# The MLP's up projection as seven Strassen block products in two passes over the tokens, with the hidden layer taken through DRAM

## The chip, the cores and the metric

One Trainium2 chip, one of its cores. The metric is the device time of one execution in microseconds, the median over runs. Engines are named as in the profile: PE is TensorE's matmuls and PEld its weight loads, DVE is VectorE, ACT is ScalarE, POOL is GpSimd, SP is the engine on whose queue the DMAs are issued. SBUF is the on-chip memory, PSUM the banks that TensorE writes to.

## The reference

One layer of an encoder in float32, model width 1024, on 256 + 1024 = 1280 tokens. A norm and an input projection feed two branches (a state-space branch S5 and a two-directional Mamba-2 branch), whose outputs are gated, merged, projected and added to the input. Then comes the part that the change touches:

```python
x = x + (merged @ w_o)
h = rmsnorm(x, norm2_w)
x = x + jnp.square(jax.nn.relu(h @ w_up)) @ w_down    # w_up 1024 x 4096, w_down 4096 x 1024
```

and a last norm.

## The kernel before, in words

Data lie with channels on the 128 partitions and tokens along the free axis, so an activation of width 1024 is 8 blocks of 128 x 1280. Matmuls keep float32 accuracy by splitting both operands: hi is the value rounded to TensorE's format (an ACT copy), lo the rest (a subtraction), and each product is three matmuls, wl x hi, wh x lo, wh x hi. `mm3` (line 132) does that for one bank of PSUM; `mm3n` (139) does it for several chunks of tokens with the same weights, each matmul with a weight load of its own. `load_w` (113) fetches 4 blocks of weights (128 x 512, 256 KB) into a `raw` tile on SP's queue, casts them to `wh` on ACT (line 119) and subtracts for `wl` (line 120) on the engine that `lows` names in turn: POOL alone, and POOL and DVE in turn from line 761 to 775. There are four buffers of wh and of wl.

The stages at the end run in this order. The S5 output stage (lines 679 to 712) works on 320 tokens at a time. Then the tokens go through in three chunks of 432, 432 and 416 (`cs`, line 669). For each, `merge` (717) projects the Mamba branch and adds the gated S5 branch; `norm_rows` (753) makes the reciprocal norm `rs2` of the chunk before, by one matmul and a chain of DVE operations (`rsqrt`, 933); `normed` (655) prepares the next chunk; and `residual` (732) multiplies by w_o, adds the input to give x2, stores x2 to DRAM and leaves hi and lo of x2 times the norm's weights in `xn` (lines 743, 744). Squares are summed on ACT and POOL (749, 750). As rs2 is one factor per token, it is applied only after the up projection.

The MLP (780 to 816) goes over 16 blocks of 256 hidden channels. `up(b)` (783) makes two hidden tiles: 8 blocks of weights by three token chunks of 512, 512 and 256, i.e. 24 groups of three matmuls; DVE takes max(0, .) times rs2 out of PSUM (791); ACT squares that to hi (793), POOL squares it too (794) and DVE subtracts for lo (795). `down(b)` (799) multiplies the two tiles by w_down and DVE adds the result to `acc` (807), eight blocks of 128 x 1280 that start as x2, loaded back from DRAM. `up(b + 1)` is issued ahead of `down(b)`. The last two blocks of down, the last norm and the output stand in lines 818 to 930.

The order of the instructions on each engine is not written out here: a planner puts them in order at build time by the order of the program and by its own estimates of durations, with what stands in `urgent()` (106) ahead of the rest; at run time each queue is worked in order. Tiles of a pool that is closed leave their memory to later pools, whose writers then wait for the last readers. Banks of PSUM come in turn from eight (`any_bank`, 150).

## Time and profile before

| | |
|---|---|
| time, median of 3 runs | 2584.03 us (2583.57 to 2584.58) |
| the profiled execution: its time, its span | 2585.0 us, 2583.2 us |
| PE busy, share of the span | 2487.1 us, 96% |
| DVE, ACT, POOL busy | 1507.5, 948.6, 701.9 us |
| granted clock, mean over the span | 0.987 |
| merge and residual, up and down, last norm | 1376 to 1664.6, to 2507, to the end |

Busy shares are averages over stages. What an engine's work costs is read in its own stage: from what TensorE waits for there, and from the rate at which its matmuls start. A matmul's recorded duration overlaps with the next one's, so durations of PE don't add up; starts do. A recorded duration on DVE or POOL holds what the instruction waited for once it had begun.

### The profile page before, as it was taken

How to read it: one execution, taken by the hardware profiler on the slowest of the kernel's cores; microseconds unless marked ns; L12 is line 12 of the kernel's file. 1: busy time of each engine (PE TensorE's matmuls, PEld its weight loads, DVE VectorE, ACT ScalarE, POOL GpSimd, SP SyncE). 2: the span in 40 equal slices, each digit the busy share in tenths (PEclk: the TensorE clock that was granted, in tenths of full speed). 3: DMA queues.
4: the chain of work that ended last, by engine and by line, in shares of the span. 5: the costliest groups of instructions: out<-in, count | busy, mean ns of one | idle time of the engine just before them, and what ended most of it. 6: DMA issues, size and time to landing. Idle time of an engine off the chain costs nothing.

```text
span 2583.2 us, 37060 instructions
## 1 busy us (share of the span) xinstructions
PE 2487.1 (96%) x14119; PEld 2132.6 (83%) x14119; DVE 1507.5 (58%) x2505; ACT 948.6 (37%) x1867; POOL 701.9 (27%) x498
## 2 busy tenths in 40 slices
PE   8999999979999999988989999999999999999998
PEld 6788878868888888877889899988888888888887
DVE  7799999682456667668653665533233333333336
ACT  7555554333545545454332444311111111111114
POOL 2521111211111111134242424432222222222235
PEclk9999999989999999989999999999999999999999
DMA  4323232333344545565656766431111111111113
GB/s 148 102 84 100 90 99 92 102 103 125 132 136 155 163 133 165 148 180 149 194 173 193 232 188 202 143 121 37 39 39 37 37 37 41 38 37 37 37 45 115
DMA packets 254434, 286.21 MB, mean 111 GB/s; under 512 B 29864, under 2 KB 186704, under 8 KB 254256
## 3 DMA queue, kind: packets, MB, share of 16 engines
q1 hardware_dynamic: 252528, 279.90, 34.5%
q10 hardware_dynamic: 1728, 3.93, 0.5%
q8 instruction: 112, 1.84, 0.3%
q14 instruction: 66, 0.54, 0.1%
HBM read 210.26 MB, written 73.50 MB: 110 GB/s over the span
## 4 chain that ended last, share of the span: by engine, by line
PE 70%; DVE 17%; DMA 6%; ACT 3%; issue 2%; SPq 1%; POOL 1%; ACTq 0%; DVEq 0%; POOLq 0%
PE pa L145 24%; PE mm L136 20%; PE pa L136 9%; PE mm L145 8%; DVE z L1184 1%; DVE z L1183 1%; PE ps L478 1%; PE y L624 1%; DMA wt<-w_d 1%; PE ba L600 1%; PE ex L611 1%; DMA raw<-w_m 1%; PE ex L613 1%; DMA ec<-es_d 1%; DVE gx L652 1%
## 5 line engine op out<-in xcount | busy, mean ns | idle before, releaser
L120 POOL TENSOR_TENSOR wl<-raw,wh 128x512 fp32r<-128x512 f32 (+1 forms) x362 | 501.9, 1390 | 1734.5 <-ACT wh L119 1656.2
L119 ACT ACTIVATE wh<-raw 128x512 fp32r<-128x512 f32 (+1 forms) x422 | 257.9, 614 | 923.0 <-PE pa L145 522.9
L136 PE MATMUL mm<-hh,wl 128*128 128x512 f32 (+1 forms) x1272 | 465.3, 366 | 15.4 <-ACT hh L223 7.2
L136 PE MATMUL mm<-hh,wh 128*128 128x512 f32 (+1 forms) x1272 | 465.5, 366 | 0.0
L136 PE MATMUL mm<-hl,wh 128*128 128x512 f32 (+1 forms) x1272 | 464.8, 365 | 0.0
L136 PEld LDWEIGHTS mm<-hh,wl 128*128 128x128 f32 x1272 | 241.7, 190 | 56.5 <-issue 7.3
L136 PEld LDWEIGHTS mm<-hl,wh 128*128 128x128 f32 x1272 | 241.8, 190 | 41.7 <-issue 3.2
L136 PEld LDWEIGHTS mm<-hh,wh 128*128 128x128 f32 x1272 | 242.0, 190 | 41.3 <-issue 4.1
L145 PE MATMUL pa<-hid,wh 128*128 128x512 f32 (+1 forms) x1008 | 254.6, 357 | 0.0
L807 DVE TENSOR_TENSOR acc<-acc,pa 128x512 f32<-128x512 f32 (+1 forms) x252 | 138.0, 593 | 140.5 <-PE pa L145 140.5
L145 PEld LDWEIGHTS pa<-hid,wh 128*128 128x128 f32 x1008 | 170.3, 188 | 29.8
L791 DVE SCALAR_TENSOR_TENSOR r<-pa,rs 128x512 f32<-128x512 f32 (+1 forms) x72 | 39.5, 595 | 230.1 <-PE pa L145 230.1
L136 PE MATMUL pa<-gx,wh 128*128 128x432 f32 (+1 forms) x576 | 158.5, 356 | 0.0
L145 PE MATMUL pa<-xnh,wl 128*128 128x512 f32 (+1 forms) x576 | 155.8, 357 | 0.0
L145 PE MATMUL pa<-xnl,wh 128*128 128x512 f32 (+1 forms) x576 | 155.0, 357 | 0.0
L145 PE MATMUL pa<-xnh,wh 128*128 128x512 f32 (+1 forms) x576 | 154.0, 357 | 0.0
L145 PE MATMUL pa<-hid,wl 128*128 128x512 f32 (+1 forms) x504 | 143.4, 355 | 0.0
L321 DVE SCALAR_TENSOR_TENSOR ac<-xpad,hcw,ac 128x1282 f32<-128x1282 f32 x60 | 93.9, 1565 | 45.4 <-ACT ac L319 45.0
L136 PEld LDWEIGHTS pa<-gx,wh 128*128 128x128 f32 x576 | 108.3, 188 | 3.6
L145 PEld LDWEIGHTS pa<-xnh,wh 128*128 128x128 f32 x576 | 96.5, 188 | 17.9
L145 PEld LDWEIGHTS pa<-xnh,wl 128*128 128x128 f32 x576 | 96.5, 188 | 17.8
L145 PEld LDWEIGHTS pa<-xnl,wh 128*128 128x128 f32 x576 | 96.4, 188 | 17.9
(458 smaller groups left out, 4881.1 us busy)
## 6 DMA issues: line engine op xcount, KB each, us to landing
raw<-w_in SPq DMA_DIRECT2D x110, 256.0 KB
raw<-w_m SPq DMA_DIRECT2D x72, 256.0 KB
raw<-w_dn SPq DMA_DIRECT2D x72, 256.0 KB
raw<-w_up SPq DMA_DIRECT2D x64, 256.0 KB
ec<-es_d SPq DMA_DIRECT2D x80, 192.0 KB
xz<-xz_d SPq DMA_DIRECT2D x40, 384.0 KB
raw<-w_o SPq DMA_DIRECT2D x48, 256.0 KB
gate_d<-gv SPq DMA_DIRECT2D x16, 640.0 KB
```

The lines of the kernel that those rows point to most:

```text
L119: act.activation(wh[:, :n], raw[:, :n], AF.Copy)
L120: lows[n_low[0] % len(lows)].tensor_tensor(wl[:, :n], raw[:, :n], wh[:, :n], SUB)
L136: pe.matmul(out, l, r[:, sl], start=(n == 0), stop=(n == last))
L145: pe.matmul(o, l, r[:, sl], start=(n == 0), stop=(n == last))
L321: dve.scalar_tensor_tensor(ac[:, :n], xp[:, k:k + n], w(k), ac[:, :n], MUL, ADD)
L478: pe.matmul(st[:, :384], xt[:, 384:512], xs, start=True, stop=True)
L600: pe.matmul(bk[:, q * P:(q + 1) * P], st[:, q * P:(q + 1) * P], cf, start=True, stop=True)
L611: pe.matmul(ps[:, d].rearrange("p (h l) -> p h l", h=3), eye, out_of[:, d:d + 1].to_broadcast([P, 3, P]), start=True, stop=False)
L613: pe.matmul(ps[:, d], el[:, d], er[:, 3 * hh_:3 * hh_ + 3].rearrange("p h l -> p (h l)"), start=False, stop=True)
L624: pe.matmul(y[e0 * 64:e0 * 64 + 64, q * P:(q + 1) * P], xt[:, h * 64:h * 64 + 64], G[h // 3][:, h % 3], start=True, stop=True)
L791: dve.scalar_tensor_tensor(r[:, s], pt, 0.0, rs2[:, s], MAX, MUL)
L807: dve.tensor_tensor(ac[:, m, s], ac[:, m, s], pt, ADD)
```

## The change

The up projection h @ w_up is done by Strassen's scheme in the form with seven products. The tokens are halved into two passes of 640 (`HT`), each again into two groups of 320 (`NQ`); the 1024 input channels into two halves of 4 blocks; the 4096 hidden channels into 16 pairs of 128-wide tiles. For each pair and pass, seven products of 4 blocks take the place of eight, each of 12 matmuls of 320 columns. Their weight operands a11, a12, s2, s3, s1, a22, s4 are formed from the four raw weight tiles on POOL and DVE and split into hi and lo each time (`part_w`); their token operands b11, b21, t2, t3, t1, t4, b22 are formed from x2 by `operands`, once per pass. For that, x2 stays in SBUF and is multiplied by the norm's weights and by rs2 first. The operands of the first pass are made inside the third residual chunk, those of the second during the first pass (b11, b21, t2) and right after it (the others, in the memory of the first pass's). Each pair's result is relu-squared and stored to DRAM (`h_d`); `hidden` loads it for the down projection, which starts only when both passes are through, starts acc by a copy, and gets x2 added later by POOL. `lows` stays at POOL and DVE in turn.

The diff, cut to its core:

```diff
+    xp = ctx.enter_context(tc.tile_pool(name="x2b", bufs=1, side="right"))
+    xa = xa_ctx.enter_context(tc.tile_pool(name="x2a", bufs=1, side="right"))
+    x2 = [[z.tile([P, HT], F32, name=f"x2{m}") for m in range(8)] for z in (xa, xp)]
+    rs2 = [z.tile([P, HT], F32, name="rs2") for z in (xa, xp)]
...
-    def residual(t0, n, mer):
+    def residual(t0, n, mer, between=None):
...
-            dve.scalar_tensor_tensor(xr, pt, 0.125, xr, MUL, ADD)
-            nc.sync.dma_start(x2_d[m, :, s], xr)
-            act.activation(xn[m][0][:, s], xr, AF.Copy, scale=V("n2w", m))
-            dve.scalar_tensor_tensor(xn[m][1][:, s], xr, V("n2w", m), xn[m][0][:, s], MUL, SUB)
...
+            for p, d, o in pieces(s):
+                z = x2[p][m][:, d]
+                dve.scalar_tensor_tensor(z, pt[:, o], 0.125, xr[:, o], MUL, ADD)
+                nc.sync.dma_start(x2_d[m, :, p * HT + d.start:p * HT + d.stop], z)
+                act.activation(sq[:, o], z, AF.Square)
+            if m:
                 pool.tensor_tensor(ss, ss, sq, ADD)
+            if between and m % 2 == 0:
+                next(between)
...
+    def operands(p, place):
+        todo = {z: [] for z in LATE}
+        ops = {z: [] for z in EARLY + LATE}
+        n = [0]
+        def put(z, src, k):
+            hi, lo = (place(f"{z}{k}{e}", z) for e in "hl")
+            act.activation(hi, src, AF.Copy)
+            n[0] += 1
+            (pool if n[0] % 2 else dve).tensor_tensor(lo, src, hi, SUB)
+            ops[z].append((hi, lo))
+        for k in range(4):
+            for m in (k, k + 4):
+                z = x2[p][m]
+                dve.scalar_tensor_tensor(z, z, V("n2w", m), rs2[p], MUL, MUL)
+            b11, b12, b21, b22 = (x2[p][m][:, o:o + NQ] for m in (k, k + 4) for o in (0, NQ))
+            put("b11", b11, k)
+            put("b21", b21, k)
+            dve.tensor_tensor(b11, b12, b11, SUB)
+            t2 = tq()
+            dve.tensor_tensor(t2, b22, b11, SUB)
+            dve.tensor_tensor(b12, b22, b12, SUB)
+            put("t2", t2, k)
+            dve.tensor_tensor(b21, t2, b21, SUB)
+            late = (("t3", b12), ("t1", b11), ("t4", b21), ("b22", b22))
+            if p == 0:
+                for z, src in late:
+                    put(z, src, k)
+            else:
+                for z, src in late:
+                    todo[z].append(src)
+            yield ops
+        for z in LATE:
+            for k, src in enumerate(todo[z]):
+                put(z, src, k)
+        yield ops
...
+            if i == 2:
+                nctx.close()
+                oa = ox.enter_context(tc.tile_pool(name="opa", bufs=1))
+                tq = lambda: oa.tile([P, NQ], F32, name="t2s", bufs=1)
             if rest:
                 norm_rows(*rest)
-            if i + 1 < len(cs):
+            if i == 2:
+                between = operands(0, lambda n, z: oa.tile([P, NQ], F32R, name=n))
+            else:
                 gx = normed(*cs[i + 1])
-            rest = residual(*c, mer)
+            rest = residual(*c, mer, between)
...
+        def part_w(src, eng):
+            wh, wl = (wp.tile([P, 4, P], F32R, name=z) for z in ("wh", "wl"))
+            with urgent():
+                act.activation(wh, src, AF.Copy)
+                eng.tensor_tensor(wl, src, wh, SUB)
+            return [(wh[:, i], wl[:, i]) for i in range(4)]
+        def up_pair(p, i, ops):
+            with urgent():
+                r = []
+                for m in (2 * i, 2 * i + 1):
+                    for k in (0, 4):
+                        raw = tp.tile([P, 4, P], F32, name="raw", bufs=6)
+                        nc.sync.dma_start(raw, a["w_up"][m][:, k:k + 4])
+                        r.append(raw)
+                a11, a12, a21, a22 = r
+                s1, s2, s3, s4 = (tp.tile([P, 4, P], F32, name="sw", bufs=5) for _ in range(4))
+            def product(src, z, eng):
+                w = part_w(src, eng)
+                pt = any_bank()[:, :NQ]
+                mm3(pt, w, ops[z], slice(0, NQ))
+                return pt
...
+            with urgent():
+                pool.tensor_tensor(s1, a21, a22, ADD)
+                dve.tensor_tensor(s2, s1, a11, SUB)
+            pt = product(a11, "b11", pool)
+            act.activation(p1, pt, AF.Copy)
+            pt = product(a12, "b21", dve)
+            dve.tensor_tensor(c1[:, n0], p1, pt, ADD)
+            pt = product(s2, "t2", pool)
+            dve.tensor_tensor(u2, p1, pt, ADD)
+            with urgent():
+                pool.tensor_tensor(s3, a11, a21, SUB)
+                dve.tensor_tensor(s4, a12, s2, SUB)
+            pt = product(s3, "t3", pool)
+            dve.tensor_tensor(u3, u2, pt, ADD)
+            pt = product(s1, "t1", dve)
+            dve.tensor_tensor(c2[:, n1], u3, pt, ADD)
+            dve.tensor_tensor(u2, u2, pt, ADD)
+            pt = product(a22, "t4", pool)
+            dve.tensor_tensor(c2[:, n0], u3, pt, SUB)
+            pt = product(s4, "b22", dve)
+            dve.tensor_tensor(c1[:, n1], u2, pt, ADD)
+            for c, m in ((c2, 2 * i + 1), (c1, 2 * i)):
+                dve.scalar_tensor_tensor(c, c, 0.0, c, MAX, MUL)
+                nc.sync.dma_start(h_d[m][p], c)
+        turn_b = operands(1, lambda n, z: (ob if z in EARLY else oa).tile([P, NQ], F32R, name=n))
+        for i in range(16):
+            up_pair(0, i, ops)
+            if i in (3, 6, 9, 12):
+                next(turn_b)
+        ops = next(turn_b)
+        for i in range(16):
+            up_pair(1, i, ops)
...
-    lows = [pool]
...
-        def up(b):
+        def hidden(b):
...
+                for p in range(2):
+                    r = xp.tile([P, HT], F32, name="hr", tag=f"x2{(4 * b + 2 * i + p) % 8}")
+                    nc.sync.dma_start(r, h_d[2 * b + i][p])
+                    s = slice(p * HT, p * HT + HT)
+                    act.activation(hi[:, s], r, AF.Copy)
+                    (pool if p else dve).tensor_tensor(lo[:, s], r, hi[:, s], SUB)
...
-        for m in range(8):
-            nc.sync.dma_start(ac[:, m], x2_d[m])
-        hid = up(0)
+        hid = hidden(0)
         for b in range(14):
-            nxt = up(b + 1)
+            nxt = hidden(b + 1)
             down(b, hid, CS)
             hid = nxt
-        hids = [hid, up(15)]
+            if 1 <= b <= 8:
+                r = tp.tile([P, NT], F32, name="r")
+                nc.sync.dma_start(r, x2_d[b - 1])
+                pool.tensor_tensor(ac[:, b - 1], ac[:, b - 1], r, ADD)
+        hids = [hid, hidden(15)]
```

## Rows read from the trace of the kernel before

**Rows 1.** The table of stretches: us, busy us of each engine, clock, DMA.
```profile
core 0: us, PE busy (x) PEld busy (x) DVE busy (x) ACT busy (x) POOL busy (x), PEclk, DMA share, GB/s
1428.00:1476.00 48.00, 42.90 (x200) 37.79 (x199) 36.90 (x50) 23.38 (x43) 21.59 (x15) 0.96 0.74 238
1476.00:1560.00 84.00, 83.84 (x428) 79.77 (x427) 52.76 (x80) 34.86 (x62) 29.18 (x19) 1.00 0.62 193
1624.00:1664.60 40.60, 40.60 (x214) 39.69 (x213) 23.69 (x36) 18.45 (x32) 19.66 (x16) 1.00 0.51 165
1664.60:1722.00 57.40, 57.40 (x294) 48.40 (x293) 18.98 (x26) 9.97 (x14) 19.61 (x13) 1.00 0.37 137
1722.00:2450.00 728.00, 728.00 (x3739) 614.59 (x3738) 248.43 (x416) 98.86 (x130) 194.83 (x130) 1.00 0.12 38
```

**Rows 2.** The page's chain that ended last, by line.
```profile
PE pa L145 24%; PE mm L136 20%; PE pa L136 9%; PE mm L145 8%; DVE z L1184 1%; DVE z L1183 1%; PE ps L478 1%; PE y L624 1%; DMA wt<-w_d 1%; PE ba L600 1%; PE ex L611 1%; DMA raw<-w_m 1%; PE ex L613 1%; DMA ec<-es_d 1%; DVE gx L652 1%
```

**Rows 3.** Timeline of PE, up projection: start, us, instruction; the first and twelfth triple.
```profile
1752.50 0.75 PE L145 MATMUL pa<-xnh,wh 128*128 128x512 f32 x3
...
1758.95 0.75 PE L145 MATMUL pa<-xnl,wh 128*128 128x512 f32 x3
```

**Rows 4.** Timeline of PE, S5 output stage: the first and the 95th of a row.
```profile
1334.72 0.31 PE L136 MATMUL mm<-sx5h,wl 128*128 128x320 f32 x1
...
1348.51 0.31 PE L136 MATMUL mm<-sx0l,wh 128*128 128x320 f32 x1
```

**Rows 5.** Timeline of POOL in the first residual stretch.
```profile
1465.44 1.10 POOL L750 TENSOR_TENSOR ss<-ss,sq 128x432 f32<-128x432 f32 x1 [2.84 <-ACT sq L749]
...
1469.63 1.28 POOL L120 TENSOR_TENSOR wl<-raw,wh 128x512 fp32r<-128x512 f32 x1
1471.39 1.11 POOL L750 TENSOR_TENSOR ss<-ss,sq 128x432 f32<-128x432 f32 x1 [0.48 <-ACT sq L749]
1472.77 1.36 POOL L120 TENSOR_TENSOR wl<-raw,wh 128x512 fp32r<-128x512 f32 x1 [0.26 <-ACT wh L119]
```

**Rows 6.** Timeline of DVE in the same stretch.
```profile
1464.88 0.67 DVE L744 SCALAR_TENSOR_TENSOR xnl<-xr,vec,xnh 128x432 fp32r<-128x432 f32 x1 [0.73 <-ACT xnh L743]
1465.46 0.60 DVE L741 SCALAR_TENSOR_TENSOR xr<-pa,xr 128x432 f32<-128x432 f32 x1
...
1470.03 1.43 DVE L120 TENSOR_TENSOR wl<-raw,wh 128x512 fp32r<-128x512 f32 x1
1471.38 1.59 DVE L744 SCALAR_TENSOR_TENSOR xnl<-xr,vec,xnh 128x432 fp32r<-128x432 f32 x1
```

**Rows 7.** Instructions of line 711, 320 wide from PSUM: min/median/max ns.
```profile
L711 DVE SCALAR_TENSOR_TENSOR t<-t,mm x32: 468/486/489, 1210.7 to 1369.7; 128x320 f32<-128x320 f32 x32
```

**Rows 8.** Groups by line and shape: out<-in, count, busy us, mean ns, idle before.
```profile
L120 POOL TENSOR_TENSOR wl<-raw,wh 128x512 fp32r<-128x512 f32 x306 | 433.2, 1418 | 1559.5 <-ACT wh L119 1481.5 <-issue 35.7 <-DMA cs_d<-dte_4966p 13.8
...
L119 ACT ACTIVATE wh<-raw 128x512 fp32r<-128x512 f32 x366 | 228.9, 628 | 884.6 <-PE pa L145 522.9 <-PE mm L145 182.8 <-PE pa L136 98.8
...
L795 DVE TENSOR_TENSOR hid<-r,hid 128x1280 fp32r<-128x1280 f32 x32 | 47.7, 1492 | 67.0 <-POOL r L794 67.0
...
L793 ACT ACTIVATE hid<-r 128x1280 fp32r<-128x1280 f32 x32 | 40.8, 1276 | 20.7 <-DVE r L791 19.2 <-POOL wl L120 1.5
```

**Rows 9.** Timeline of DVE, the norm of tokens 432 to 863.
```profile
1629.39 0.60 DVE L758 TENSOR_SCALAR ss<-mm 128x432 f32<-128x432 f32 x1
...
1631.46 1.71 DVE L939 TENSOR_TENSOR ln<-ln,ss 128x432 f32<-128x432 f32 x1
1633.20 0.61 DVE L940 SCALAR_TENSOR_TENSOR rs<-ln,rs 128x432 f32<-128x432 f32 x1
...
1636.16 1.71 DVE L938 SCALAR_TENSOR_TENSOR ln<-rs 128x432 f32<-128x432 f32 x1
...
1639.98 0.59 DVE L940 SCALAR_TENSOR_TENSOR rs<-ln,rs 128x432 f32<-128x432 f32 x1
```

**Rows 10.** Waits of SP's queue, 1376 to 2507 us: total us, times, longest.
```profile
SPq L118 <- POOL wl L120: 839.5, 160, 9.6
```

49 lines of the change are left out of this document (29 added, 20 removed).

## The prediction

> **What bounds the kernel now.** I read the time by stage first, as the change touches one stage. [...]
>
> TensorE's price comes from the timeline of its starts. In the up projection a group of three matmuls (512+512+256 columns) starts every (1758.95-1752.50)/11 = 0.586 us, 0.458 ns a column [rows 3]. The S5 stage has the width the change wants: 320 columns, one matmul every 13.79/94 = 0.1467 us, again 0.458 ns a column [rows 4]. A narrower matmul with a weight load of its own is thus no dearer per column.
>
> [...]
>
> The next view is the one that matters: POOL and DVE side by side, where both are busy [rows 5, 6]. At 1469.63 POOL begins a subtraction (1.28 us, ends 1470.91). DVE begins one with two SBUF inputs at 1470.03 and takes 1.43 us (one at 1464.88, 432 wide and with POOL idle, 0.67): it ends 0.55 us after POOL. At 1471.38 the same (1.59 us, 0.47 after POOL's end), and POOL's own from 1472.77 ends 1.16 us after that. But DVE's operation that reads PSUM (1465.46, 0.60 us) runs unhindered beside POOL's of 1465.44. So POOL's operations and DVE's with two SBUF inputs exclude each other; in turns they hold that shared path for about 1.15 us (POOL, 512 wide), 0.98 (432), and 0.55 (512) or 0.47 (432) on DVE. Scaled by width (estimates): POOL 320 wide 0.73; DVE 640 wide 0.68, 320 wide 0.35.
>
> [...]
>
> **TensorE's part.** Up projection now: 32 tiles x 8 blocks x 3 = 768 groups x 0.5864 = 450.4 us. After: 2 passes x 16 pairs x 7 products x 12 = 2688 matmuls x 0.1467 = 394.3 us; 12.3 us a pair. **-56**.
>
> **The shared path, per pair.** Weights are split seven times a pair and pass instead of four times a pair in all (224 splits, before 64), and sums of blocks come on top. POOL: four subtractions for weights and s1, s3: 6 x 1.15 = 6.9 us. DVE: three weight subtractions, s2, s4: 5 x 0.55, two squarings of 640: 2 x 0.68; 4.1 us. Path: 11.0 us of TensorE's 12.3 (89%). The seven additions from PSUM (0.49 us each [rows 7]) don't take the path but stand in DVE's queue: DVE 7.5 us. ACT: 7 x 0.63 [rows 8] and one 320-wide copy, about 0.5: 4.9 us. Four weight buffers let the splits run up to four products (7 us) ahead. Pass 2: 176 us of path, plus 8.6 of late operands, against 197: fits, but tighter than anything here (residual's last 37 us ran without a TensorE pause on 29 of path: weights and sums 20.5, xn 3.8, a norm 5; worked out below). **+4** for hiccups, 0 to 12.
>
> Pass 1 also carries the second half's operands: 8 scalings of 640, 20 differences, 12 low parts: 19 us of path; with the last norm (5) 176+24 = 200 us against 197. Path-bound, and with 3% lost to order **+9**; 0 if POOL slips in wherever DVE reads PSUM, 25 at 90% use.
>
> **Start of pass 1.** Now the first up matmul follows the residual without a pause, since xn needs no norm. After, the operands need rs2 of the first 864 tokens. That chain runs from 1629.39 to 1640.57, stretched by POOL (two of its steps take 1.71 us where the others take 0.6) [rows 9]. From there residual has 24 us left, in which its own path work is some 12 us: 16 weight subtractions (8 x 1.15 + 8 x 0.55) and 7 sums of squares (0.98) are 20.5, some 8 of it done by then; xn's 8 x 0.47 leaves. The operands bring 8 x 0.68 + 20 x 0.35 + 14 x 0.35 + 14 x 0.73 = 27.5 us. So 39.5 in 24: product one, which needs b11 of all four blocks, starts **+15** late; low end 5 (the planner puts late operands behind), high end 25 (weight splits queue behind them too). ACT's 28 casts fit.
>
> **Between the passes.** t3, t1, t4, b22 of pass 2 lie in pass 1's buffers and wait for pair 15's products, but have 10 us until needed: 16 casts, 8.6 us of path on a full queue: **+3**, 0 to 8.
>
> **Into the down projection.** Now hid is ready a whole block ahead. After, hid's memory is that of pass 2's last operands, so cast and subtraction follow the last product: 640-wide cast about 0.65 us and subtraction 0.75 to 1.4 (half of 1280 wide [rows 8], or POOL), plus signalling: **+4**, 0 to 8. Then the down blocks run back to back with less side work than before (r*r gone, loads and copies instead, 28 us a block): nothing.
>
> **Transfers.** w_up is loaded twice, h written and read: a pair moves 1.05 MB in and 0.66 out in 12.3 us, 138 GB/s; the merge runs at 193 to 238 [rows 1]. On SP's queue 64 more weight loads, 64 h stores and 64 loads come; a store waits for DVE's squaring and weight loads may stand behind it, covered by six raw buffers (one and a half pairs). Today SP waits for buffers to come free (839.5 us on POOL's subtraction [rows 10]), not for transfers: 0, and if the cover goes, up to 1 us a pair, which is inside the ends above. acc's load from x2 becomes eight POOL additions under down blocks: 0. Down's weight subtractions alternate on DVE, the end with them: **+2**, -1 to 5.
>
> **Sum.** -56+15+9+3+4+4+2 = -19 on the profiled 2585.0 us (span 2583.2, 1.8 around it), 2566; the median, 2584.0, lies 1 below: **2565**. All ends low give 2532, all high 2611.
>
> **Rivals.** *The path never binds* (POOL works while DVE reads PSUM, operands spread out): only the transitions remain, about +12, giving 2540. For it: 89%, and no TensorE pause at 80% today. Against: the start's 39.5 in 24 us is hard to spread. 18%.
>
> *The path becomes the bound*, the slower side. Place: both passes and the residual's end. From 1628 us, 53 (norm 5, weights and sums 20.5, operands 27.5) + 32 x 11.0 + 33 (later operands 28, norm 5) = 438 us of path stand against TensorE's 431 to the end of pass 2 at 2059. The forecast's +31 until there means that the path is used at 95%. At 91% pass 2 ends at 2109, and with the 6 us behind it the gain of 56 is gone: that is the point from which this case decides. At 88% it ends at 2126 and the time is about **2600**. For it: both queues are in order, the planner orders by its own durations, and a DVE operation that waits for PSUM holds up those behind it. Against: with two queues full, one takes the path as the other leaves it [rows 5, 6]. 24%.
>
> *The narrow matmuls cost more*, so that the products don't get seven eighths of the time: 10 ns on each of 2688 is 27 us and gives 2592, but rows 4 show the very width within 1 ns of rows 3's price per column; 2%. [...] A lower granted clock where TensorE pauses (0.96 at 1428 to 1476 us [rows 1]) is 4% of 394 us at most and inside the range.
>
> **Numbers.** Forecast 56% (own range 2550 to 2583), path hidden 18%, path-bound 24%, narrow 2%. 0.2% (5.2 us) is about what a measurement here can tell from no change. Faster by more: all of the hidden case, nearly all of the forecast, a little of the third, 0.73; within: 0.09; slower 0.18. Range 2538 to 2596 leaves out the path-bound tail and the best case's edge.
>
> **What would show it.** Right: 320-column starts every 0.147 us in the passes; a TensorE pause of 10 to 20 us (or slow residual) ahead of the first product with POOL and DVE both near 9 tenths; pass 1 longer than pass 2; POOL's mean for weight subtractions above 1.42 us [rows 8]; 197 to 205 us for pass 2; a short pause before the first down block. Wrong: TensorE without pauses in pass 1 while POOL waits for ACT (path hidden), or TensorE waiting for wl throughout both passes (path-bound), or for raw (transfers).

## The result: 0.7% slower, where 0.7% faster was forecast

The changed kernel takes 2604.63 us (median of 4 runs, 2601.51 to 2605.93); the kernel before, timed beside it, 2584.31 us (4 runs). The ratio is 1.0072, 95% interval 1.0059 to 1.0085. That lies outside the predicted range (2538 to 2596) and on the other side, and is near the 2600 that the rival "the path becomes the bound" gave.

The page of the kernel after, its busy times (total, share, count) and the chain that ended last by line [rows 2]:

```profile
PE 2454.9 (94%) x14503; PEld 2156.8 (83%) x14503; DVE 1925.3 (74%) x2957; ACT 1071.9 (41%) x2131; POOL 921.6 (35%) x626
...
PE pa L146 11%; PE pa L137 4%; PE mm L146 4%; DVE wl L853 1%; DVE c L897 1%; DVE sw L877 1%; PE mm L137 1%; DVE c L890 0%; DVE c L895 0%; DVE c L893 0%; DVE u L891 0%; PE mm L961 0%; POOL wl L853 0%; PE mm L976 0%; DMA h<-c 0%
```

TensorE works 32 us less than before (2487.1 us) over a span that is 16.5 us longer (2599.7 against 2583.2). VectorE's busy time rose from 1507.5 to 1925.3 us, and for the first time lines of VectorE in the MLP (`wl` L853, `c` L897, `sw` L877) stand in the chain. The table of stretches, with the columns of [rows 1], shows where:

```profile
1624.00:1664.60 40.60, 33.10 (x163) 30.99 (x163) 40.39 (x50) 18.65 (x39) 24.58 (x20) 0.96 0.34 111
1664.60:1700.00 35.40, 12.20 (x38) 9.45 (x36) 32.74 (x43) 9.71 (x21) 17.87 (x15) 0.55 0.24 81
1700.00:1800.00 100.00, 91.07 (x588) 88.84 (x588) 97.44 (x116) 34.81 (x61) 72.94 (x46) 0.96 0.33 119
...
1950.00:2110.00 160.00, 157.26 (x1048) 153.50 (x1048) 157.64 (x173) 58.91 (x99) 126.12 (x77) 1.00 0.38 135
```

Before, TensorE had every microsecond from 1624 to 2450 us, at a granted clock of 1.00 [rows 1], so there the columns it was fed were the time. Now it is VectorE that is busy from 92% to over 99% from 1624 us to the end of pass 2, and TensorE that has gaps, in the second row above all: 12.20 of 35.4 us, at a granted clock of 0.55. The timeline of TensorE names what it waited for (its waits of over 5 us and some shorter ones stand here, and two more starts of the first product):

```profile
1645.74 0.46 PE L137 MATMUL pa<-mer,wl 128*128 128x416 f32 x1 [3.33 <-POOL wl L121]
...
1650.08 0.46 PE L137 MATMUL pa<-mer,wl 128*128 128x416 f32 x1 [1.79 <-DVE wl L121]
...
1676.09 1.76 PE L767 MATMUL mm<-ss,cst 128*128 128x416 f32 x2 [2.98 <-POOL ss L759]
1690.07 0.64 PE L137 MATMUL mm<-b110h,wl 128*128 128x320 f32 x1 [12.22 <-POOL wl L853]
1690.50 0.47 PE L137 MATMUL mm<-b110l,wh 128*128 128x320 f32 x1
...
1693.17 0.47 PE L137 MATMUL mm<-b113h,wh 128*128 128x320 f32 x1
1699.03 0.64 PE L137 MATMUL pa<-b210h,wl 128*128 128x320 f32 x1 [5.40 <-DVE wl L853]
...
1711.64 0.63 PE L137 MATMUL pa<-t10h,wl 128*128 128x320 f32 x1 [5.68 <-DVE wl L853]
...
2132.19 0.77 PE L146 MATMUL mm<-hid,wl 128*128 128x512 f32 x1 [6.24 <-ACT hid L925]
```

The starts of 1690.50 and 1693.17 are ten matmuls apart: 0.267 us each, against 0.1467 in [rows 4]; TensorE had stood still for 12.22 us, and the mean granted clock of 1690 to 1700 us is 0.50. From about 1719 us on the price of [rows 4] holds (pair 1's twelve starts of its first product, 1718.87 to 1720.49 us, are 0.147 us apart): the granted clock of 1719 to 1733 us is 1.00.

From such starts the span can be taken apart. In both kernels the last chunk's residual begins with its first matmul on `mer`:

| | before | after | difference | forecast |
|---|---|---|---|---|
| to the first `mer` matmul of the last chunk | 1627.85 | 1621.39 | -6.5 | 0 |
| from there to the first up matmul | 36.8 | 68.7 | +31.9 | +15 |
| up projection, pass 1 | | 224.1 | | |
| up projection, pass 2 (to 2125.95) | | 211.8 | | |
| up projection, sum | 450.4 | 435.9 | -14.5 | -56+9+3+4 = -40 |
| wait into the down projection | 0 | 6.2 | +6.2 | +4 |
| down, last norm, output | 468.1 | 467.5 | -0.6 | +2 |
| span | 2583.2 | 2599.7 | +16.5 | -19 |

The -6.5 is not to be read as a gain: in the profiled runs of those experiments that leave the code ahead of it as it is, the same matmul starts anywhere from 1620.1 to 1630.8 us. Below, stretches are therefore measured from that start.

**Inside a pair.** One pair of pass 2 (12.76 us from s2 to s2), VectorE's timeline and then GpSimd's, which answer to [rows 5, 6]:

```profile
2040.27 1.77 DVE L877 TENSOR_TENSOR sw<-sw,raw 128x512 f32<-128x512 f32 x1
2041.96 1.78 DVE L853 TENSOR_TENSOR wl<-sw,wh 128x512 fp32r<-128x512 f32 x1
2043.78 1.66 DVE L886 TENSOR_TENSOR sw<-raw,sw 128x512 f32<-128x512 f32 x1
...
2048.45 0.69 DVE L853 TENSOR_TENSOR wl<-raw,wh 128x512 fp32r<-128x512 f32 x1
2049.05 0.48 DVE L893 TENSOR_TENSOR c<-u,pa 128x320 f32<-128x320 f32 x1
2049.56 1.71 DVE L897 SCALAR_TENSOR_TENSOR c<-c 128x640 f32<-128x640 f32 x1
2051.19 0.47 DVE L895 TENSOR_TENSOR c<-u,pa 128x320 f32<-128x320 f32 x1
2051.70 1.41 DVE L897 SCALAR_TENSOR_TENSOR c<-c 128x640 f32<-128x640 f32 x1
2053.03 1.78 DVE L877 TENSOR_TENSOR sw<-sw,raw 128x512 f32<-128x512 f32 x1
...
2041.57 1.63 POOL L885 TENSOR_TENSOR sw<-raw 128x512 f32<-128x512 f32 x1
2043.16 3.44 POOL L853 TENSOR_TENSOR wl<-raw,wh 128x512 fp32r<-128x512 f32 x2
2049.29 1.29 POOL L876 TENSOR_TENSOR sw<-raw 128x512 f32<-128x512 f32 x1 [2.69 <-DVE wl L853]
```

VectorE never stands idle here: each instruction starts as the one before it ends. But s2, `wl` and s4 take 1.66 to 1.78 us where the same form takes 0.69 at 2048.45 (and 0.68 to 0.69 with GpSimd out, experiment 2), because GpSimd's operations run at the time (`sw` at 2041.57 ends at 2043.20, VectorE's `wl` of 2041.96 0.54 us later, as in [rows 5, 6]). Such waiting of VectorE for a running GpSimd instruction is called a hold below. Its reads of PSUM (0.47 to 0.49 us, [rows 7]) are untouched. So it is full, in part with waiting that is recorded as work. That TensorE gets its weights at VectorE's pace (pairs 18 to 31 take 12.83 us each in place of TensorE's 12.32) is the reading that the experiments test.

The norm of tokens 432 to 863 [rows 9] runs from 1622.94 to 1636.4 us, two of its steps again at 1.71 us. GpSimd's weight subtractions went, as forecast, above the 1418 ns of [rows 8]: 1796 ns from sums and 1727 ns from raw blocks. SP's queue no longer stands for 839.5 us as in [rows 10]; from 1376 to 2510 us its longest entry is:

```profile
SPq L119 <- POOL wl L121: 212.4, 70, 8.9
```

### The profile page after: what moved, and what is told of

Read it like the earlier page. It is cut to its first block, busy times and chain, and to the rows that moved or that the text cites. A ratio compares the mean times of both kernels' runs of the same rounds, so it can differ in the third digit from the quotient of the medians.

```text
span 2599.7 us, 39693 instructions
## 1 busy us (share of the span) xinstructions
PE 2454.9 (94%) x14503; PEld 2156.8 (83%) x14503; DVE 1925.3 (74%) x2957; ACT 1071.9 (41%) x2131; POOL 921.6 (35%) x626
## 5 line engine op out<-in xcount | busy, mean ns | idle before, releaser
L121 POOL TENSOR_TENSOR wl<-raw,wh 128x512 fp32r<-128x512 f32 (+1 forms) x262 | 370.6, 1418 | 1351.0 <-ACT wh L120 1250.6
L120 ACT ACTIVATE wh<-raw 128x512 fp32r<-128x512 f32 (+1 forms) x358 | 217.9, 610 | 481.1 <-PE pa L146 176.0
L939 DVE TENSOR_TENSOR acc<-acc,pa 128x512 f32<-128x512 f32 (+1 forms) x234 | 128.0, 593 | 107.0 <-PE pa L146 107.0
L852 ACT ACTIVATE wh<-sw 128x512 fp32r<-128x512 f32 x128 | 80.7, 632 | 153.4 <-PE pa L137 112.4
L121 DVE TENSOR_TENSOR wl<-raw,wh 128x512 fp32r<-128x512 f32 x96 | 76.7, 799 | 58.8 <-ACT wh L120 58.4
L853 POOL TENSOR_TENSOR wl<-sw,wh 128x512 fp32r<-128x512 f32 x64 | 113.8, 1796 | 11.5 <-ACT wh L852 11.5
L853 POOL TENSOR_TENSOR wl<-raw,wh 128x512 fp32r<-128x512 f32 x64 | 109.5, 1727 | 5.1 <-ACT wh L852 5.1
L137 PE MATMUL pa<-mer,wh 128*128 128x432 f32 (+1 forms) x384 | 107.9, 363 | 0.0
L137 PE MATMUL pa<-gx,wl 128*128 128x432 f32 (+1 forms) x288 | 103.3, 359 | 1.4 <-POOL wl L121 1.4
L852 ACT ACTIVATE wh<-raw 128x512 fp32r<-128x512 f32 x96 | 60.5, 632 | 102.3 <-PE pa L137 47.1
```

Of the source, the lines that this page charges most:

```text
L120: act.activation(wh[:, :n], raw[:, :n], AF.Copy)
L121: lows[n_low[0] % len(lows)].tensor_tensor(wl[:, :n], raw[:, :n], wh[:, :n], SUB)
L137: pe.matmul(out, l, r[:, sl], start=(n == 0), stop=(n == last))
L852: act.activation(wh, src, AF.Copy)
L853: eng.tensor_tensor(wl, src, wh, SUB)
L939: dve.tensor_tensor(ac[:, m, s], ac[:, m, s], pt, ADD)
```

## The experiments

All are edits of the kernel after, except where said; each ratio is to the kernel before, timed beside it on the same chip. The kernel after stands at 1.0072, so 0.001 of the ratio is 2.6 us. Times of one stage come from the starts of TensorE's matmuls. A is from the first `mer` matmul of the last chunk to the first product of pass 2, B from there to the first matmul of the down projection; the last column is the mean from the start of pair 18 to that of pair 31. The number in brackets behind a run is that of its experiment below; the run of 2 has no ratio and is not in the table.

| run | ratio (95% interval) | A us | B us | pairs 18 to 31, us each |
|---|---|---|---|---|
| after | 1.0072 (1.0059 to 1.0085) | 292.8 | 218.0 | 12.83 |
| square on ScalarE (1) | 1.0007 (0.9999 to 1.0016) | 283.1 | 211.9 | 12.43 |
| raw memory (3) | 1.0057 (1.0045 to 1.0069) | 292.4 | 217.8 | 12.81 |
| second half later (4) | 1.0087 (1.0072 to 1.0101) | 296.3 | 217.9 | 12.82 |
| hid memory (5) | 1.0055 (1.0041 to 1.0069) | 293.0 | 212.8 | 12.84 |
| early norm (6) | 1.0055 (1.0042 to 1.0068) | 289.0 | 217.7 | 12.82 |
| four moves (5) | 0.9974 (0.9963 to 0.9984) | 280.3 | 203.6 | 12.32 |
| four moves, early norm (6) | 0.9961 (0.9948 to 0.9974) | 273.0 | 204.4 | 12.38 |
| scalings spread (7) | 0.9979 (0.9969 to 0.9989) | 279.8 | 203.4 | 12.32 |
| scalings spread, sum memory (8) | 0.9947 (0.9931 to 0.9963) | 270.2 | 203.7 | 12.32 |
| GpSimd's sum twice (9) | 1.0210 (1.0191 to 1.0229) | 307.9 | 236.7 | 13.98 |
| raw eight (10) | 1.0043 (1.0031 to 1.0056) | 290.4 | 211.4 | 12.64 |
| GpSimd constant (10) | 1.0134 (1.0119 to 1.0150) | 309.7 | 217.7 | 12.80 |
| raw eight, GpSimd constant (10) | 1.0102 (1.0088 to 1.0116) | 307.8 | 210.6 | 12.51 |

The theory once the two traces were compared: VectorE's queue is the bound of the passes, made full by its holds for GpSimd. The rivals: that the weights come late (memory, transfers), that the order of the second half's operands costs the time, that TensorE's narrow matmuls do.

**1. The squares of a pair go to ScalarE.**

```diff
-                dve.scalar_tensor_tensor(c, c, 0.0, c, MAX, MUL)
+                act.activation(c, c, AF.Relu)
+                act.activation(c, c, AF.Square)
```

> The changed kernel with the pair's relu and square (two DVE operations of 640 with two SBUF inputs, 1.52 us each in the trace) made by ACT instead (relu, then square). Shared-path theory (POOL's operations and DVE's with two SBUF inputs exclude each other, which fills DVE's queue): the pair's period falls from 12.8 us to 12.3 to 12.4 in pass 2 and from 13.1 to about 12.6 in pass 1, 15 to 20 us less in all, about 2587 us; the start of pass 1 stays as it is. Rival (each product costs something of its own, a new bank or the first matmul's wait): the period stays at 12.8 and the time within 3 us of 2604.6.

Measured: 2589.83 us, 0.65% below the kernel after (17 us). Pairs 1 to 15 fell from 13.0 to 12.43 us. The row of pass 2 in its table of stretches:

```profile
1950.00:2110.00 160.00, 160.00 (x1093) 160.00 (x1092) 129.27 (x159) 92.94 (x156) 106.93 (x76) 1.00 0.38 130
```

TensorE has no gap in these 160 us, VectorE is at 81%. Taking two instructions a pair from VectorE (ScalarE does their work in four) returned the steady pairs' time; nothing else was moved. Pair 0 stayed at 28.2 us and the start before it at 68.6.

**2. GpSimd out of the passes.** Its weight subtractions are replaced by a constant tile, s1 and s3 by raw blocks (`a21`, `a11`).

```diff
-                eng.tensor_tensor(wl, src, wh, SUB)
+                if eng is pool:
+                    wl = w0
+                else:
+                    eng.tensor_tensor(wl, src, wh, SUB)
...
-                s1, s2, s3, s4 = (tp.tile([P, 4, P], F32, name="sw", bufs=5) for _ in range(4))
+                s2, s4 = (tp.tile([P, 4, P], F32, name="sw", bufs=5) for _ in range(2))
+                s1, s3 = a21, a11
```

> The changed kernel without POOL's work on the up projection's weights: wl of the four products that POOL serves is a constant tile, and s1 and s3 are left out (a21 and a11 stand in their place), so part of the computation is missing; DVE's and ACT's work is all there. Shared-path theory: DVE's operations with two SBUF inputs fall to what they take alone (squaring of 640 about 0.8 us instead of 1.52, 512-wide sums and subtractions 0.7 instead of 1.4 to 1.7), DVE is busy about 60% of the passes, and the pair's period is 12.3 to 12.4 us in pass 2. Rival (DVE's operations are slow for another reason, the DMA traffic or TensorE's reading): they stay above 1.2 us.

Measured: 2570.14 us (one run), with TensorE busy for 200.00 of the 200 us from 1700 on and 130.00 of the 130 from 1950 on. VectorE has all its operations left. Its groups by line and shape in 1950 to 2080 us, first of the kernel after (square, s2, s4, an addition from PSUM):

```profile
L897 DVE SCALAR_TENSOR_TENSOR c<-c 128x640 f32<-128x640 f32 x21 | 32.8, 1562 | 0.7
...
L877 DVE TENSOR_TENSOR sw<-sw,raw 128x512 f32<-128x512 f32 x11 | 19.6, 1778 | 0.0
L886 DVE TENSOR_TENSOR sw<-raw,sw 128x512 f32<-128x512 f32 x10 | 16.6, 1664 | 0.3
...
L890 DVE TENSOR_TENSOR c<-u,pa 128x320 f32<-128x320 f32 x8 | 3.9, 489 | 0.7
```

and then the same four without GpSimd:

```profile
L903 DVE SCALAR_TENSOR_TENSOR c<-c 128x640 f32<-128x640 f32 x20 | 16.4, 822 | 0.3
...
L884 DVE TENSOR_TENSOR sw<-raw 128x512 f32<-128x512 f32 x10 | 6.9, 693 | 3.2 <-DMA raw<-w_up 2.7
L892 DVE TENSOR_TENSOR sw<-raw,sw 128x512 f32<-128x512 f32 x10 | 6.8, 684 | 0.0
L890 DVE TENSOR_TENSOR u<-p,pa 128x320 f32<-128x320 f32 x9 | 4.4, 488 | 10.8 <-PE pa L137 10.8
```

The square takes 822 in place of 1562 ns, s2 and s4 690 in place of 1778 and 1664; the addition from PSUM stays. Of a pair's VectorE work, 2 x 0.82 + 5 x 0.69 + 7 x 0.49 = 8.5 us, the rest up to 12.8 is waiting for GpSimd. The up projection takes 406.1 us there (first matmul at 1687.96, end of the last at 2094.06) in place of 435.9, and pass 2, from 1896.68, 197.4: TensorE's own time. The start stays long, 64.3 us in place of 68.7. As this is one run with part of the work left out, these times show where the time goes and not what a usable kernel would take.

**3. The raw weight tiles in memory of their own.** In the kernel after the first load of w_up is issued at 1685.00 us, as the last chunk's norm ends: its tile has the norm's old memory.

```diff
+                ur = ox.enter_context(tc.tile_pool(name="upraw", bufs=6))
...
-                        raw = tp.tile([P, 4, P], F32, name="raw", bufs=6)
+                        raw = ur.tile([P, 4, P], F32, name="raw", bufs=6)
```

> The changed kernel with the six raw tiles of the up projection in memory of their own beside the first pass's operands, so that w_up's first loads no longer wait for the residual's last norm to leave that memory. Memory theory (the first load, issued at 1685.0 us after 10.3 us of waiting, is what makes the first product late): the first product starts 8 to 12 us earlier and the time falls by 6 to 10 us. Order theory (the second pass's scalings and differences stand ahead of pair 0's weight work in DVE's queue): the first product comes earlier, but the products behind it wait longer, and the time falls by 3 us at most.

Measured: 2603.02 us. The first product started 11 us earlier (1679.3), but the third then waited, and pass 1 ended where it had (1914.1 us). TensorE's row and GpSimd's:

```profile
1700.78 0.64 PE L137 MATMUL pa<-t20h,wl 128*128 128x320 f32 x1 [18.13 <-POOL wl L854]
...
1687.35 1.91 POOL L877 TENSOR_TENSOR sw<-raw 128x512 f32<-128x512 f32 x1 [7.96 <-issue]
```

GpSimd's s1 (L877) stood for 7.96 us with nothing that the profile names: its tile too had memory of the norm. What this wait costs in the kernel with the other moves stands in 8.

**4. The second half's operand work behind the pair's last addition.**

```diff
-                next(turn_b)
+                with tc.issue_after(last[0].ins):
+                    next(turn_b)
```

> The changed kernel with each part of the second pass's operands queued on DVE behind the last addition of the pair after which the program writes it (pairs 3, 6, 9, 12), so that the planner can't put it ahead of pair 0. Order theory: the waits of 5.4 and 5.7 us ahead of pair 0's second and fifth product go, the first product stays where it is or comes a little earlier, pairs 3 to 12 get 0 to 8 us longer: 4 to 11 us less in all. Memory theory alone: no change beyond 3 us. Shared-path theory alone (only the sum of the work counts): no change beyond 3 us.

Measured: 2612.96 us, 4 us above the kernel after. Pair 0 took 16.5 us in place of 28.8, and pairs 1 to 15 took 14.1 in place of 13.0. The order moved the time from the first pair to the later ones.

**5. Together: the square on ScalarE, raw memory, the order of 4, and the hidden tiles of `hidden` in memory of their own; and the last of these alone.**

```diff
+        hp2 = mctx.enter_context(tc.tile_pool(name="hidp", bufs=8, side="right"))
...
-                hi, lo = (tp.tile([P, NT], F32R, name="hid", bufs=8) for _ in range(2))
+                hi, lo = (hp2.tile([P, NT], F32R, name="hid", bufs=8) for _ in range(2))
```

> Together: the square of a pair on ScalarE, the raw weight tiles in memory of their own, the second half's operand work behind the pair's last addition, the hidden tiles in memory of their own. Sum theory (VectorE's own queue with its waits for GpSimd sets the passes; a move pays only once the queue has slack): with the square gone there is slack of some 30 us in 160, so the moves that gained nothing alone now pay: first product about 11 us earlier and pair 0 about 10 us shorter, of which half is kept, and the 6 to 7 us wait into the down projection goes: 2570 to 2580, that is 10 to 20 us below the square alone (2589.8). Rival (the moves are worthless in any case, because the operand work of the first pairs is itself the bound at the start): only the last wait goes, 2583. Second rival (weights of a pass arrive too late): no change from the square alone, 2590.

> After with the hidden tiles in memory of their own, nothing else. Theory (the wait into the down projection is for the memory of pass 2's last operands): the wait of 6.24 us falls under 1 us, 2598.5. Rival (it is for the last store of the hidden rows to DRAM and their way back, which no memory shortens): no change, 2604.

Measured: 2579.91 us together, 0.26% below the kernel before. The four ratios' shares alone (-16.8, -3.9, +3.9, -4.4 us) add up to -21; together they give -25, so the raw memory and the order gained little even with slack in VectorE's queue: by the ratios the run lies 8.5 us below the square alone, under the 10 to 20 of the sum theory. The hidden tiles alone: the wait into the down projection fell from 6.24 to 0.61 us and B from 218.0 to 212.8; the time, 2601.94, by 4.4 us. That wait was for memory.

**6. The third chunk's norm and the first half's eight scalings in the third merge**, alone and on top of 5.

```diff
+            if hook and m == 1:
+                hook()
...
+        def first_half():
+            norm_rows(*rest)
+            for m in range(8):
+                z = x2[0][m]
+                dve.scalar_tensor_tensor(z, z, V("n2w", m), rs2[0], MUL, MUL)
```

> After with the normalisation of the third chunk and the first half's eight scalings in the third merge, nothing else. Sum theory: 12 to 16 us of VectorE's work leave the stretch from 1624 us on, in which VectorE is busy 98%, and TensorE's pauses shrink by most of that: 2590 to 2596. Rival (own chain of the last chunk): the waits of the residual stage go (about 8 us of them) but the pause ahead of the first product stays, and the passes start less than 5 us earlier: 2600 to 2604.

> As the run of four moves, and the second-half chunk's first norm scalings (the first half's eight scalings and the normalisation of the third chunk) taken into the third merge, ahead of the residual stage of the last chunk. Sum theory: some 12 to 16 us of VectorE leave the stretch in which TensorE waits most (1624 to 1700 us), so about 8 to 12 us less than the run of four moves: 2560 to 2570. Rival (TensorE's pause there is set by the last chunk's own chain of matmul, residual, sum of squares, norm, first scaling, and not by VectorE's sum): under 3 us less.

Measured: 2602.89 alone and 2580.24 on top. Both miss what the sum theory said. In the run alone A fell by 3.8 us, but in the third merge (1554 to 1624.6 us) TensorE's busy time fell from 70.38 to 67.29 us, and the pause stayed:

```profile
1690.25 0.64 PE L137 MATMUL mm<-b110h,wl 128*128 128x320 f32 x1 [12.17 <-POOL wl L863]
```

On top of 5, A fell by 7.3 us and the same stretch of the merge lost 3.4 (70.60 to 67.23 us). There the pause stands ahead of the third product (10.55 us, for GpSimd's `wl`), where it stood before (9.99 us). So here the rival was nearly right (by the ratios 3.4 us less on top of 5): the pause is set by the last chunk's own norm and what waits for it, which 3 and 8 show to be memory for a part, and the merge gave its room at a price.

**7. The second half's eight scalings one behind each of the pairs 0 to 7**, on top of 5, with the rest of the second half back in the order of after. In the kernel after they stand in a row ahead of pair 0's weights (VectorE's timeline of after; the first row is the first half's, inside the last residual):

```profile
1636.43 9.94 DVE L797 SCALAR_TENSOR_TENSOR x<-x,vec,rs 128x640 f32<-128x640 f32 x8
...
1684.96 9.15 DVE L797 SCALAR_TENSOR_TENSOR x<-x,vec,rs 128x640 f32<-128x640 f32 x8
```

```diff
+                if p == 0:
+                    dve.scalar_tensor_tensor(z, z, V("n2w", m), rs2[p], MUL, MUL)
...
+            if i < 8:
+                m = i // 2 + 4 * (i % 2)
+                with tc.issue_after(last[0].ins):
+                    dve.scalar_tensor_tensor(x2[1][m], x2[1][m], V("n2w", m), rs2[1], MUL, MUL)
```

> As the run of four moves, but the second half's operand work is back in the order of after, except its eight norm scalings, which come one behind each of the pairs 0 to 7. Theory (the first pair is held up by work placed ahead of it, the later pairs by work placed into them in bursts): pair 0 as in the run of four moves (about 25 us), pairs 1 to 15 at 12.5 us as with the square alone in place of 13.26, so pass 1 212 us in place of 222.7 and the time 2568 to 2573. Rival (the operand work of the second half costs its time wherever it stands): pass 1 stays over 219 us and the time over 2577.

Measured: 2581.40 us, pass 1 222.2 us. The rival held: 222.7 before this edit, so the operand work of the second half costs its time in pass 1 whether it comes in bursts or spread.

**8. The sums s1 to s4 in memory of their own**, on top of 7.

```diff
+                us = ox.enter_context(tc.tile_pool(name="upsw", bufs=4))
...
-                s1, s2, s3, s4 = (tp.tile([P, 4, P], F32, name="sw", bufs=5) for _ in range(4))
+                s1, s2, s3, s4 = (us.tile([P, 4, P], F32, name="sw", bufs=4) for _ in range(4))
```

> As the run with the scalings spread, and the tiles of the sums s1 to s4 in memory that is open before the last residual stage (four buffers in place of five). Theory (in the run of four moves GpSimd's first sum stood still for 7.96 us until the last chunk's norm was over, since its tile reuses the norm's memory; the third product waits 9.99 us for it): the third product comes 7 to 9 us earlier, and the time is 6 to 9 us below the run with the scalings spread, 2560 to 2566. Rival (VectorE's norm work itself is what stands in front): under 2 us. Second rival (four buffers hold the sums of the next pair up): slower than the run with the scalings spread, with pairs over 12.6 us.

Measured: 2574.99 us, ratio 0.9947 (0.9931 to 0.9963): the fastest of all, 0.5% below the kernel before and 1.2% below the kernel after. By the ratios it is 8 us below 7, as the theory said; A fell by 9.6 us, B not at all. TensorE's rows, and one of ScalarE:

```profile
1676.22 0.46 PE L137 MATMUL pa<-mer,wl 128*128 128x416 f32 x1 [3.23 <-DVE wl L121]
...
1679.92 0.47 PE L137 MATMUL pa<-b210h,wl 128*128 128x320 f32 x1
...
1681.91 0.31 PE L137 MATMUL pa<-t20h,wl 128*128 128x320 f32 x1
...
1706.34 0.64 PE L137 MATMUL mm<-b210h,wl 128*128 128x320 f32 x1 [8.43 <-ACT p L884]
...
1705.85 0.77 ACT L884 ACTIVATE p<-mm 128x320 f32<-128x320 f32 x2 [7.21 <-DVE rs L772]
```

The products of pair 0 now run while the residual ends (b21 at 1679.92, t2 at 1681.91, with the last `mer` matmuls from 1676.22), where the third product had waited 9.86 us. What is left stands in the last two rows: 8.43 us for the norm of the last chunk, now inside pair 1. TensorE waits there for ScalarE to read the first product out of PSUM, and that copy (`p1`) waits for the norm's last instruction (`rs`), whose result it does not use. So a third tile, `p1`, seems to lie in memory that the norm still holds; no run has moved it. The second rival (four buffers) did not show: pairs 18 to 31 stay at 12.32 us.

**9. One more GpSimd sum per pair, a11 - a21, into a tile that nobody reads.**

```diff
+                pool.tensor_tensor(tp.tile([P, 4, P], F32, name="spare", bufs=1), a11, a21, SUB)
```

> After with one more GpSimd sum in each pair (a11 - a21 once more, into a tile that nobody reads); it stands in no chain of results. Theory (GpSimd's holds block VectorE's operations with two inputs in SBUF, and VectorE's queue is 98% full): each pair gets 0.8 to 1.2 us longer, pass 2's pairs 13.6 to 14.0 us in place of 12.83, the whole 25 to 38 us, 2630 to 2643. Rival (VectorE's own work is the bound, and GpSimd, 79% busy, takes one more operation in its idle time): pairs under 13.0 us, the whole under 6 us, below 2611.

Measured: 2639.64 us, pairs 13.98, in the numbers just what the theory said, but the trace shows another way there. VectorE's s2 and GpSimd's extra sum in 1950 to 2080 us:

```profile
L877 DVE TENSOR_TENSOR sw<-sw,raw 128x512 f32<-128x512 f32 x9 | 15.9, 1769 | 9.9 <-POOL sw L876 9.9
...
L886 POOL TENSOR_TENSOR spare<-raw 128x512 f32<-128x512 f32 x10 | 13.9, 1387 | 20.5 <-DMA raw<-w_up 20.5
```

The extra sum waited 20.5 us for raw blocks, with s1 behind it in the queue, and VectorE stood idle 9.9 us for s1. TensorE's waits from 1950 to 2110 us, 12.2 us, are for GpSimd's weight subtractions in the main (9.3). So the run opened a second rival: six raw buffers are a ring (s4 frees a12, whose buffer takes the next a22, which s1 needs), and that ring might set the pace in the kernel after too. Two edits part them.

**10. Eight raw buffers; the extra GpSimd subtraction on a constant tile; both.**

```diff
-                        raw = tp.tile([P, 4, P], F32, name="raw", bufs=6)
+                        raw = tp.tile([P, 4, P], F32, name="raw", bufs=8)
```

```diff
+                pool.tensor_tensor(tp.tile([P, 4, P], F32, name="spare", bufs=1), w0, w0, SUB)
```

> After with eight raw weight buffers in place of six, nothing else: the next pair's four blocks can be loaded while this pair's are still read. Theory (in the passes VectorE's queue is the bound: in after it stands idle 0.7 us or less per group in 130 us, and its operations are stretched by GpSimd's holds): pairs 18 to 31 stay at 12.7 to 12.9 us, the whole within 3 us of after. Rival (the ring of raw buffers is the bound: s4 frees a12, whose buffer is loaded with the next a22, which s1 waits for; GpSimd's s1 waits up to 2.8 us for that load): pairs fall to 12.4 us, the whole to 2585 to 2592.

> After with one more GpSimd subtraction per pair, on a constant tile, so that no weight buffer is held longer by it (in the run with the sum twice the extra sum also read a11 and a21 and stood in the queue behind their loads, and VectorE waited up to 2.8 us for s1). Theory (GpSimd's holds stretch VectorE's operations, and its queue is full): pairs 13.2 to 13.9 us, the whole 12 to 35 us over after, 2616 to 2640. Rival (what cost there was the longer hold of the raw buffers): pairs at 12.8 to 12.95, under 4 us over after, 2605 to 2609.

> Eight raw buffers and the extra GpSimd subtraction on a constant tile together. Theory: as the run with the constant alone, 2616 to 2640, since neither the buffers nor their loads set the pace. Rival (the ring of raw buffers): as the run with eight buffers alone, within 4 us of it.

Measured: 2598.32, 2621.36 and 2612.76 us, the last between its two forecasts. Eight buffers gain 7.5 us by the ratios and pairs of 12.64 us, between the two forecasts: the ring has a share, 0.2 us, in the 0.5 us that a pair loses there; the rest goes, by 1 and 2, to VectorE's queue with its holds. VectorE's s4 no longer meets GpSimd there (692 ns), while s2 and the square still do:

```profile
L897 DVE SCALAR_TENSOR_TENSOR c<-c 128x640 f32<-128x640 f32 x20 | 32.8, 1640 | 0.3
...
L877 DVE TENSOR_TENSOR sw<-sw,raw 128x512 f32<-128x512 f32 x10 | 17.6, 1765 | 8.9 <-POOL wl L853 8.9
...
L886 DVE TENSOR_TENSOR sw<-raw,sw 128x512 f32<-128x512 f32 x11 | 7.6, 692 | 0.4
```

The constant subtraction is held by no buffer, so the order put all 32 of them into the first ten pairs. The list of the tile's instructions, and the row of the table of stretches where they lie:

```profile
L888 POOL TENSOR_TENSOR spare<-w x32: 1029/1483/1710, 1690.7 to 1835.8; 128x512 f32<-128x512 f32 x32
...
1700.00:1800.00 100.00, 80.26 (x482) 77.28 (x482) 93.93 (x107) 30.48 (x54) 89.14 (x61) 0.90 0.29 97
```

No engine waits for these 32 results but ScalarE once, for 1.2 us, and GpSimd had 27% of that stretch free in the kernel after. Still the first ten pairs took 162.1 us in place of 146.6, A grew by 16.9 us and the whole by 16. With eight buffers the same 32 cost 15 us (by the ratios). So the cost, 0.5 us for each operation of about 1.5 us, does not need the ring. But it is not shown to be the hold on VectorE, which the theory was about. What TensorE waits for in the first ten pairs, first in the kernel after and then with the constant (products in the banks `pa`: us in total, times, longest):

```profile
PE pa L137 <- POOL wl L853: 1.1, 2, 0.6
...
PE pa L137 <- POOL wl L855: 9.5, 9, 2.3
```

Its waits for VectorE's subtractions hardly change (14.0 and 15.4 us), and VectorE is busy 91% of these pairs in place of 97%, GpSimd 89% in place of 74%. So here GpSimd's own queue is full, and the weight subtractions that TensorE needs stand in it behind the extra ones. That VectorE is slowed by holds rests on 1 and 2. Pass 2, which has none of the 32, stays at 12.80.

## Why the prediction was wrong

Numbers in brackets are those of the experiments.

**Where the miss lies.** The span came out some 36 us above the forecast (+16.5 in place of -19). Against their terms the start took 16.9 us more, pass 1 18.0, the change of passes and pass 2 7.7, the way into the down projection 2.2; the stages ahead and behind give 9.1 back. So two terms failed, "Start of pass 1" (+31.9 in place of +15, range 5 to 25) and pass 1's "with 3% lost to order +9" (+27.0, range 0 to 25). The others stayed inside their ranges. The steady pairs alone (1 to 15 and 17 to 31) lost 18 us, where the two passes had been given 9 + 4. What had no term is pair 0, 16.5 us.

**TensorE's price: right.** 320-column matmuls keep the price of [rows 4] in the passes: with VectorE's queue relieved, pairs take 12.32 us (84 matmuls at 0.1467), as forecast, and nothing of the "narrow matmuls" rival shows.

**The shared path: the mechanism right, the bound wrong.** The step that failed behind both terms is that the path can be kept 95% busy, since "with two queues full, one takes the path as the other leaves it". By the prediction's own 438 us of path over the 503 us from the norm at 1622.94 to the end of pass 2, the path was used 87%; the rival "the path becomes the bound" took 88%. By stage: 53 of 67.1 us (79%) to the first product, 200 of 224.1 (89%) in pass 1, 184.6 of 211.8 (87%) in pass 2. (The prediction counts 20 differences for each half of the tokens, where the code has 16; at 0.35 us each that is 1.4 us a half and changes none of this.) The quoted sentence was true of two instructions of [rows 5, 6] and not of 32 pairs: GpSimd stands 2.7 us a pair without work, as s1 waits for a raw block or for VectorE (GpSimd's s1 in the kernel after, 1950 to 2080 us, ten pairs):

```profile
L876 POOL TENSOR_TENSOR sw<-raw 128x512 f32<-128x512 f32 x10 | 12.9, 1294 | 27.2 <-DMA raw<-w_up 16.4 <-DVE wl L853 10.7
```

The same holds for "The seven additions from PSUM ... don't take the path but stand in DVE's queue: DVE 7.5 us". The prediction held the path (11.0 us) and VectorE's queue (7.5 us) against TensorE's 12.3 one by one. But the queue is in order: while VectorE waits for GpSimd it does not read PSUM either (in the pair shown above s2, `wl` and s4 fill 5.1 us from 2040.27 on, where they take 2.1 alone (2), and the next read of PSUM starts at 2045.37). Its own work is 8.5 us (2), and with its holds it fills the 12.8 us that TensorE's pairs took. So the rival was right, in number and in mechanism, but for one of its reasons: VectorE does not wait for PSUM in the kernel after (idle 0.7 us or less in the rows of 2). The same s4 takes 1664 ns beside GpSimd's operations and 684 without them (2); no run here shows which read or write of an instruction makes the other engine wait.

**Pass 1: +27 in place of +9** (224.1 against 197.1; range 0 to 25). Pair 0 alone gave 16.5 of it: 11.1 us of waits (5.40 and 5.68 in the rows above), most of the rest at the lower granted clock (0.67 over 1690 to 1719 us). The forecast spread the second half's operands over the pass; the order put its eight scalings in a row (9.15 us, rows in 7) ahead of pair 0's weights. Pairs 1 to 15 took 13.0 us, 0.7 over TensorE's. Experiment 4 shows that order only shifts the time between pair 0 and the later ones; with the square gone (1) the later ones took 12.43, and with GpSimd's weight work gone (2) the pass took 208.7.

**Between the passes and pass 2: +14.7 in place of +7** (211.8 against 197.1). Pair 16 took 19.6 us, 7.3 over, where 3 (0 to 8) were forecast; the rest is 0.5 us a pair, the same full queue.

**The start: +31.9 in place of +15** (range 5 to 25). Seen rightly: operand work in VectorE's and GpSimd's queues inside the residual. The forecast's high end ("weight splits queue behind them too") came: the eight scalings (9.94 us in a row at 1636.43) and the differences and low parts behind them stand among the residual's own weight subtractions, and TensorE waits 10.1 us in five places already there (1621.4 to 1674 us):

```profile
PE pa L137 <- DVE wl L121: 6.8, 4, 2.6
PE pa L137 <- POOL wl L121: 3.3, 1, 3.3
```

Left out: that raw blocks and s1 lie in memory which the last norm still holds, so that the first product, which needs no later norm than that of tokens 432 to 863, waits for the last chunk's norm as well (12.22 us). The step "Transfers ... 0" counted the moves on SP's queue but not when their tiles come free. Moving the raw tiles alone brought the first product 11 us earlier but the time only 4 us down (3), at the edge of what a measurement can tell; s1's memory is worth 8 us in the kernel that has the other moves (8).

**Into the down projection: +6.2, forecast +4 (0 to 8)**, and by the stated mechanism: with other memory the wait is 0.61 us. **Down and the end: -0.6, forecast +2.**

Of the forecast's signs of "right" the price of a start, the pause ahead of the first product, the longer pass 1 and the short pause ahead of the down projection came; GpSimd near 9 tenths (17.87 of 35.4 us) and 197 to 205 us for pass 2 did not. Of its signs of "wrong", TensorE waited for `wl` at places throughout both passes. What stays open is how much of A each of its pauses is worth by itself, since experiments 3, 4, 6 and 7 show that a pause removed there mostly comes back at a later product. In the fastest kernel (8) A is still 270.2 us, 36 above the 36.8 + 197.1 that TensorE's work alone would take, and no run removes that.

## What to carry to other kernels

Where two engines exclude each other, add up one engine's whole in-order queue: its own operations, those that don't collide too, plus its waits for the other's; a comparison of the shared resource and of each engine alone with TensorE's time is too kind (here 11.0 and 7.5 us against 12.3, and pairs of 12.83). If that sum comes near TensorE's time, move an elementwise step to an engine that the two don't slow (here ScalarE, whose weight casts take 632 ns before, in the residual, and 632 to 633 in the passes of the kernel after: two VectorE instructions a pair, done there as four, for 17 us), before trying orders. Price the first pair of such a stage by itself, with what the order puts ahead of it: here it and the start made 33 of the 36 us by which the forecast was missed. And when a stage takes over memory from the stage before, ask for each of its first tiles who last reads that memory: tiles in memory that was free earlier gave 4 us (at the edge of what can be told), 4 and 8 at three places here.

## What was not expected of the hardware

A GpSimd operation whose result nobody needs cost 0.5 us for each of 32, although GpSimd had a quarter of the stretch free before: its own queue became what TensorE waits for. How much the two queues collided in these runs depended on how they fell against each other, and not only on how much work they held: in experiment 8 VectorE's s2 and s4 take 678 and 691 ns (1950 to 2080 us), in 7, with the same operations, 1664 and 1671, and in 1 1771 and 1673 (1950 to 2110 us). TensorE is the bound in 7 and 8 (pairs of 12.32 us), so there it is free; in the kernel after, where s2 and s4 take 1778 and 1664 ns, it is not (12.83). Last, the same code ahead of the change reached the last residual at times 10 us apart from one profiled run to another, so for a change of less than 1% only stretches measured from a common start can be compared.
